# Two small opening loads issued from ScalarE's DMA queue instead of SyncE's

## The chip, the cores and the metric

The kernel runs on one core of a Trainium2 chip. The metric is the device time of one execution in microseconds (us). Before the change the median of three runs is 630.89 us (629.98 to 631.63). The profiled execution whose trace is read below took 630.4 us, of which 628.6 us lie between its first and its last instruction (its span).

## The reference

One layer of a latent generator, for 1024 latent tokens and 256 context tokens of width 1024. A conditioning vector gives shift, scale and gate of an adaptive norm; the normed tokens go through one wide input projection, whose columns feed a neighbourhood attention and a gated short convolution; an output projection and the residual follow.

```python
def adaln(cond, w_ada, b_ada):
    m = jax.nn.silu(cond) @ w_ada + b_ada
    return jnp.split(m, 3, axis=-1)
...
    shift, scale, gate = adaln(c, w_ada, b_ada)
    shift_c, scale_c, gate_c = adaln(c_ctx, w_ada, b_ada)
    h = rmsnorm(x, norm_g) * (1 + scale[:, None]) + shift[:, None]
    hc = rmsnorm(ctx, norm_g) * (1 + scale_c) + shift_c
    q, k, v, za, u, bg, cg, zc = jnp.split(h @ w_in, SPLIT_POINTS, axis=-1)
    ...
    attn = neighbourhood_attention(q, k, heads(v), kc, vc, rpb) * jax.nn.silu(za)
    conv = gated_short_conv(u, bg, cg, zc, conv_w, conv_b)
    x_new = x + gate[:, None] * (jnp.concatenate([attn, conv], axis=-1) @ w_out)
```

## The kernel before

Everything is one long program without loops on the chip. Products are made of high and low halves in three matmuls (`mm3`), so TensorE has most of the work. The stages are: the opening (modulation, norms, transposes of `x`, and the first projection columns, up to about 60 us), the rest of the projection (to about 300 us), attention with convolution work filled in between, and the output projection.

The change lies in the opening. There each engine's order is the order of the code (`strict` chains each engine's instructions). What matters of it:

- `vec` holds 56 rows of 128 numbers: the conditioning vectors, the norm gain, biases and convolution weights. `ci` holds the 128x128 identity and two more columns. Both are loaded once, at lines 117 and 118.
- `load_slab(m, j)` loads a block of `w_ada` (`slab`). The first two blocks come as two halves each, so four transfers of 512 KB open the stream; then come tiles of `x` (`xx`, 512 KB each) and pieces of `w_in` (`wr`, 192 KB).
- On TensorE, `keep_clock(6)` runs six matmuls on zeros (`warm`); then one transpose of `vec` with the identity of `ci` writes `tr` (called `pv` in the code); then `keep_clock(7)` runs seven more; then `products(0, 0)` and `products(0, 1)` multiply the first blocks of `w_ada` with the conditioning vector.
- VectorE copies the transposed `vec` to `vecT`; ScalarE makes the SiLU of the conditioning vectors from it (`c2`, and its copies `c4` and `c0`), which the products need.
- ScalarE squares each tile of `x` with a running sum (`square`, tile `sqj`), VectorE and GpSimd make the inverse root (`root`, tile `xss`), VectorE scales the tile in place (`norm`, `xx<-xx,xss`), TensorE transposes it with the identity (`tr<-ci,xx`), ScalarE and VectorE apply the modulation (`turn`, writing `h` and `hw`), and `first_columns` makes the first projection matmuls (`acc<-h,w`).
- `row_copy(0)` on VectorE (`rw<-tr`) takes the products out of PSUM, between the first and the second `root`; `modulation(0, rw)` turns the row (`tr<-ci,rw`) and writes `ab`, which `turn` needs.

Each transfer counts up one of eight shared completion counters, and a transfer is issued only when the earlier one on its counter has landed; a counter is given to each transfer when the program is built. So at most eight of these transfers are under way.

```python
    vec = cp.tile([P, P], F32, name="vec")
    nvec = vecs.shape[0]
    sp.dma_start(vec[:nvec], vecs)
    sp.dma_start(ci, cst[:, 0:P + 2])
...
    load_slab(0, 0)
    load_slab(0, 1)
    load_x(range(4))
    load_chunks([0])
```

Of the kernel before, what the change touches and what calls it, by code (L numbers as in the profile page):

```python
# [19 lines left out]
P = 128  # L20
# [19 lines left out]
def body(tc, es, x, ctxt, w_ada, b_ada, w_in, q_g, k_g, rpbr, w_out, vecs, cst, out):  # L40
# [21 lines left out]
    pe, act, dve, pool = every = [ordered(e) for e in (nc.tensor, nc.scalar, nc.vector, nc.gpsimd)]  # L62
    sp = ordered(nc.sync)
# [48 lines left out]
    ci = cp.tile([P, P + 2], F32, name="ci")  # L112
    ident = ci[:, 0:P]

    vec = cp.tile([P, P], F32, name="vec")
    nvec = vecs.shape[0]
    sp.dma_start(vec[:nvec], vecs)
    sp.dma_start(ci, cst[:, 0:P + 2])
    few = cp.tile([P, 8], F32, name="few")
    pool.memset(few[:, 0:4], -0.5)  # L120
    pool.memset(few[:, 4:5], 1.0)
# [1427 lines left out]
```

## Time and profile before

| quantity | value |
|---|---|
| median of three runs | 630.89 us (629.98 to 631.63) |
| the profiled execution | 630.4 us |
| its span, first to last instruction | 628.6 us |
| TensorE busy (matmul) | 621.7 us, 99% |
| VectorE busy | 433.5 us, 69% |
| ScalarE busy | 326.5 us, 52% |
| DMA queue of SyncE (q1) | 97516 packets, 114.24 MB |
| DMA queue of ScalarE (q10) | 6208 packets, 11.05 MB |

PE is TensorE's matmul side and PEld its weight loads; DVE is VectorE, ACT ScalarE, POOL GpSimd. SPq and ACTq rows are DMA instructions in the queues of SyncE and ScalarE; the time of such a row is the time that issuing takes, not the transfer's. A matmul's row gives its time from start to end, and matmuls overlap, so the step from one start to the next is shorter than a row's mean. Most instructions are emitted through one helper and stand under L55; they are told apart by the tiles. A bracket at the end of a row gives how long the engine stood idle before it and what ended that.

### The profile page before, as it was taken

What the parts mean: (1) busy time and instruction counts of PE and PEld (TensorE: products, weight loads), DVE (VectorE), ACT (ScalarE), POOL (GpSimd) and SP (SyncE); (2) the same over time, 40 slices, a digit from 0 to 9 for tenths busy, and PEclk for the clock granted to TensorE, in tenths of its full rate; (3) what the DMA queues carried; (4) which work ended last, traced back from release to release, by engine and by line L of the source; (5) the groups of instructions that cost most, each with busy time, mean ns of one, the idle gap of its engine ahead of it and who ended that gap; (6) DMA issues with size and microseconds to landing.
All of it is one profiled execution on the core that took longest, in us unless ns stands there. A gap on an engine that the chain in (4) does not pass through costs nothing.

```text
span 628.6 us, 10005 instructions
## 1 busy us (share of the span) xinstructions
PE 621.7 (99%) x3487; PEld 538.5 (86%) x3488; DVE 433.5 (69%) x889; ACT 326.5 (52%) x712; POOL 77.6 (12%) x102
## 2 busy tenths in 40 slices
PE   8999999999999999999999999999999999999998
PEld 3577899999999999888888888888888888888887
DVE  1887858866866855568897879988998865594111
ACT  3777835524625545346576568566774845450000
POOL 1305014113223221100000000000000002004200
PEclk9999999999999999999999999999999999999999
DMA  8983737967784995885474553775542235963621
GB/s 316 347 282 124 178 111 259 286 204 244 236 293 137 302 320 181 298 264 214 144 238 140 192 172 127 214 254 181 190 136 76 61 93 163 357 226 121 213 102 50
DMA packets 104030, 126.45 MB, mean 201 GB/s; under 512 B 10689, under 2 KB 70553, under 8 KB 102700
## 3 DMA queue, kind: packets, MB, share of 16 engines
q1 hardware_dynamic: 97516, 114.24, 55.3%
q10 hardware_dynamic: 6208, 11.05, 5.6%
q0 software_dynamic: 256, 0.54, 0.3%
q8 instruction: 27, 0.44, 0.3%
q14 instruction: 23, 0.19, 0.1%
HBM read 89.04 MB, written 39.04 MB: 204 GB/s over the span
## 4 chain that ended last, share of the span: by engine, by line
PE 96%; DMA 2%; SPq 1%; ACT 0%; issue 0%; DVE 0%; ACTq 0%
PE pu L55 29%; PE pacc L55 21%; PE po L55 8%; PE acc L55 6%; PE pout L75 5%; PE pout L74 5%; PE pout L76 5%; PE tr L55 4%; PE cacc L55 4%; PE pss L55 3%; PE pc L55 2%; PE pmx L55 2%; DMA xx<-in_x 2%; PE trA L55 1%; PE trB L55 1%; SPq L55 1%
## 5 line engine op out<-in xcount | busy, mean ns | idle before, releaser
L55 PE MATMUL pu<-h,uh 128*128 128x512 f32 x544 | 170.0, 394 | 0.0
L55 PE MATMUL pacc<-w,h 128*128 128x384 f32 x768 | 138.4, 337 | 0.0
L55 PEld LDWEIGHTS pacc<-w,h 128*128 128x128 f32 x768 | 132.7, 188 | 0.2
L55 PEld LDWEIGHTS pu<-h,uh 128*128 128x128 f32 x544 | 97.6, 188 | 16.8 <-ACT zs L55 0.2
L55 PE MATMUL pu<-h,ul 128*128 128x512 f32 x272 | 106.6, 392 | 0.0
L55 PEld LDWEIGHTS pu<-h,ul 128*128 128x128 f32 x272 | 51.1, 188 | 11.2
L55 POOL TENSOR_TENSOR ss<-ss,few 128x4 f32<-128x4 f32 (+1 forms) x40 | 41.9, 1049 | 124.8 <-DVE ss L55 124.8
L75 PE MATMUL pout<-wol,yh 128*128 128x512 f32 (+2 forms) x136 | 51.6, 379 | 0.0
L74 PE MATMUL pout<-woh,yh 128*128 128x512 f32 (+2 forms) x136 | 51.5, 379 | 0.0
L76 PE MATMUL pout<-woh,yl 128*128 128x512 f32 (+2 forms) x136 | 50.8, 379 | 0.0
L55 PE MATMUL acc<-h,w 128*128 128x512 f32 x144 | 38.1, 404 | 0.8 <-ACT h L55 0.8
L55 ACT ACTIVATE sq<-pacc 128x256 f32<-128x256 f32 x32 | 12.4, 388 | 47.5 <-PE pacc L55 43.7
L55 DVE TENSOR_REDUCE rm<-pmx 128x2 f32<-128x256 f32 (+1 forms) x33 | 13.8, 417 | 32.7 <-PE pmx L55 32.6
L55 ACT COPY mg<-pmx 128x256 f32<-128x256 f32 (+1 forms) x33 | 12.1, 366 | 46.4 <-PE pmx L55 42.0
L55 DVE TENSOR_TENSOR mx<-mx,sb 128x372 f32<-128x372 f32 (+2 forms) x64 | 31.9, 498 | 1.9
L55 PE MATMUL po<-phl,v 128*65 128x276 f32 (+2 forms) x192 | 32.0, 269 | 0.0
L55 DVE TENSOR_REDUCE ss<-sq 128x4 f32<-128x260 f32 (+1 forms) x40 | 15.7, 392 | 23.6 <-ACT sq L55 23.6
L55 ACT ACTIVATE qn<-pacc,ss 128x64 f32<-128x64 f32 x128 | 30.2, 333 | 3.0 <-POOL ss L55 3.0
L55 PEld LDWEIGHTS acc<-h,w 128*128 128x128 f32 x144 | 25.5, 188 | 6.5 <-ACT h L55 1.2
L1479 DVE TENSOR_TENSOR ot<-pout,xr 128x512 f32<-128x512 f32 (+2 forms) x9 | 5.7, 632 | 35.4 <-PE pout L76 33.3
L55 ACT COPY sc<-pc 128x512 f32<-128x512 f32 x32 | 18.8, 589 | 21.1 <-PE pc L55 21.0
L74 PEld LDWEIGHTS pout<-woh,yh 128*128 128x128 f32 x136 | 25.6, 188 | 4.7
(159 smaller groups left out, 1194.4 us busy)
## 6 DMA issues: line engine op xcount, KB each, us to landing
uraw<-in_w_in SPq DMA_DIRECT2D x34, 256.0 KB
q_d<-qs SPq DMA_DIRECT2D x32, 256.0 KB
k_s<-k_d SPq DMA_DIRECT2D x8, 1024.0 KB
q_s<-q_d SPq DMA_DIRECT2D x16, 512.0 KB
wr<-in_w_in SPq DMA_DIRECT2D x40, 192.0 KB
slab<-in_w_ada SPq DMA_DIRECT2D x6, 1024.0 KB
v_d<-vs SPq DMA_DIRECT2D x20, 260.0 KB
v<-v_d SPq DMA_DIRECT2D x16, 325.0 KB
```

The costliest lines, as they stand in the source:

```text
L55: i = emit(*a, **kw)
L74: i = pe.matmul(ps, ah, bh, start=first, stop=False)
L75: pe.matmul(ps, ah, bl, start=False, stop=False)
L76: pe.matmul(ps, al, bh, start=False, stop=last)
L1479: dve.tensor_tensor(ot[:, c], ps[c.start][:, c], xr[:, c], ALU.add)
```

## The change

The two small loads, of `vec` and of `ci`, are issued by ScalarE instead of SyncE. Sizes, destinations and everything behind them stay.

```diff
     vec = cp.tile([P, P], F32, name="vec")
     nvec = vecs.shape[0]
-    sp.dma_start(vec[:nvec], vecs)
-    sp.dma_start(ci, cst[:, 0:P + 2])
+    act.dma_start(vec[:nvec], vecs)
+    act.dma_start(ci, cst[:, 0:P + 2])
     few = cp.tile([P, 8], F32, name="few")
```

First, SyncE's queue at the program's start, before the change. `slab` is a block of `w_ada`, `xx` a tile of `x`, `wr` a piece of `w_in`; "waits DMAHW0" means that the transfer is issued when the earlier one on counter 0 has landed.

```order
L117 DMA vec_113<-in_vecs 56x128
L118 DMA ci_112<-in_cst 128x130
L55 DMA slab_156<-in_w_ada 128x4x256 x2
L55 DMA slab_159<-in_w_ada 128x4x256 x2
L55 DMA xx_162<-in_x 128x1024
L55 DMA xx_164<-in_x 128x1024
L55 DMA xx_166<-in_x 128x1024 [waits DMAHW0_49]
L55 DMA xx_168<-in_x 128x1024 [waits DMAHW1_49]
L55 DMA wr_170<-in_w_in 128x3x128 [waits DMAHW2_49]
L55 DMA xx_172<-in_x 128x1024 [waits DMAHW3_49]
```

And the same queue after the change:

```order
L55 DMA slab_156<-in_w_ada 128x4x256 x2
L55 DMA slab_159<-in_w_ada 128x4x256 x2
L55 DMA xx_162<-in_x 128x1024
L55 DMA xx_164<-in_x 128x1024
L55 DMA xx_166<-in_x 128x1024 [waits DMAHW0_49]
L55 DMA xx_168<-in_x 128x1024 [waits DMAHW1_49]
L55 DMA wr_170<-in_w_in 128x3x128 [waits DMAHW2_49]
L55 DMA xx_172<-in_x 128x1024 [waits DMAHW3_49]
```

The two small loads are gone from the head, and the first block of `w_ada` stands first. The waits read alike, but the counters behind them are dealt out anew: before, counters 0 to 5 went to `vec`, `ci` and the four halves of the blocks in that order; now `vec` has 0, the halves of the first block 1 and 2, `ci` 3, and the halves of the second block 4 and 5. So the fourth tile of `x` (`xx_168`) now waits for the first half block instead of for `ci`, the first `wr` for the second half block instead of the first, and the fifth tile (`xx_172`) for `ci` instead of the second half block.

Second, ScalarE's queue from its start, before:

```order
L124 ACT_TABLE_LOAD
L124 CAST oner_119<-few_116 128x1 [waits Pool_49]
L55 ACT_TABLE_LOAD
L55 ACTIVATE c2_125<-vecT_124 128x2x8 [waits DVE_49]
L55 CAST c4_211<-c2_125 128x8x2 [waits Activation_49]
```

And after:

```order
L117 DMA vec_113<-in_vecs 56x128
L118 DMA ci_112<-in_cst 128x130
L124 ACT_TABLE_LOAD
L124 CAST oner_119<-few_116 128x1 [waits Pool_49]
L55 ACT_TABLE_LOAD
L55 ACTIVATE c2_125<-vecT_124 128x2x8 [waits DVE_49]
L55 CAST c4_211<-c2_125 128x8x2 [waits Activation_49]
```

The two loads stand ahead of both table loads and of the SiLU `c2`; they wait for nothing. The order on TensorE, VectorE and GpSimd is the same as before.

## The prediction

> **What bounds the kernel now.** I read the page first, then busy time by stage, then the chain of waits through the opening, then single engines there. The page says how much each engine works:
>
> ```profile
> span 628.6 us, 10005 instructions
> PE 621.7 (99%) x3487; PEld 538.5 (86%) x3488; DVE 433.5 (69%) x889; ACT 326.5 (52%) x712; POOL 77.6 (12%) x102
> ```
>
> TensorE (PE) has work almost always. Busy time in stretches (start:end, length, then each engine) says where it has not:
>
> ```profile
> 0.00:20.00 20.00, 17.27 (x71) 6.74 (x72) 5.26 (x17) 9.44 (x17) 4.41 (x12) 1.00 0.91 335
> 20.00:60.00 40.00, 39.23 (x228) 28.42 (x228) 32.17 (x54) 28.98 (x43) 10.47 (x11) 1.00 0.67 231
> 60.00:160.00 100.00, 99.96 (x569) 92.95 (x568) 72.60 (x177) 51.50 (x155) 22.71 (x33) 1.00 0.70 211
> ```
>
> From 60 us PE is full: 99.96 of 100 us. A shift of its start is therefore handed on to the end one to one; nothing later has time to absorb it. The opening is another matter: part of the 17.27 us there are zeros that only keep PE going. The chain of waits shows what really sets it (start, length, what):
>
> ```profile
> 0.75 0.46 SPq L117
> ...
> 1.26 0.37 SPq L118
> ...
> 1.67 0.43 SPq L55
> ...
> 5.10 9.96 DMA xx<-in_x
> ...
> 15.14 1.16 ACT sqj L55 x2
> ...
> 20.03 0.79 ACT h L55
> ...
> 20.86 4.58 PE acc L55 x18
> ```
>
> The two small loads stand at the head of this chain, then SyncE's other issues, then 9.96 us in which a tile of `x` waits its turn and comes in, then squares, modulation, and at 20.86 the first projection matmuls. The last columns of the stretches are the busy share of the DMA engines and GB/s:
>
> ```profile
> 2.20:2.90 0.70, 0.70 (x3) 0.29 (x2) 0.00 (x0) 0.68 (x2) 0.00 (x0) 1.00 0.58 117
> 3.30:4.00 0.70, 0.70 (x2) 0.00 (x0) 0.00 (x0) 0.22 (x1) 0.00 (x0) 1.00 0.87 259
> 6.00:11.00 5.00, 5.00 (x24) 1.85 (x23) 0.00 (x0) 0.00 (x0) 0.00 (x0) 1.00 1.05 390
> 21.00:28.00 7.00, 7.00 (x30) 4.05 (x30) 6.14 (x12) 4.33 (x9) 2.77 (x3) 1.00 1.10 380
> ```
>
> While the small loads run, around 2.5 us, the engines carry 117 GB/s; once the blocks of `w_ada` flow they are full, at 380 to 390 GB/s, until 28 us. So the opening is a stream of bytes at full rate, and what counts is when that stream begins.
>
> **What the change gives.** SyncE issues its first block at 1.67 us; with the small loads gone it can at 0.75, where the first of them stood. That is 0.92 us. The bytes of the two loads still have to be moved, and now beside the blocks instead of ahead of them:
>
> ```profile
> ci<-in_cst SPq DMA_DIRECT2D x1, 65.0 KB
> vec<-in_vecs SPq DMA_DIRECT2D x1, 28.0 KB
> ```
>
> 93 KB at 390 GB/s are 0.24 us. The stream is thus ahead by 0.92 - 0.24 = 0.68, say 0.7 us. Behind it the new counters change little: `xx_168` now waits for a half block, but by then six transfers of 512 KB are under way, 1.3 us each at 390 GB/s, so the engines don't run dry. I count that at nothing; the cover is those six transfers.
>
> [...]
>
> **What the change costs.** First ScalarE. Its rows at the start:
>
> ```profile
> 0.74 1.28 ACT L124 ACT_TABLE_LOAD   x1 [0.74 <-PEq L1532]
> 2.24 1.28 ACT L55 ACT_TABLE_LOAD   x1
> 4.69 0.22 ACT L55 ACTIVATE c<-vecT 128x16 f32<-128x16 f32 x1 [1.17 <-DVE vecT L55]
> ...
> 12.59 1.06 ACT L55 ACTIVATE sqj<-xx 128x1024 bf16<-128x1024 f32 x1 [7.33 <-DMA xx<-in_x]
> ```
>
> Two issues, 0.46 + 0.37 us plus gaps by SyncE's rows, push the table loads back by some 0.92 us. ScalarE was free at 3.52 and is now free at 4.44, while the SiLU starts at 4.69: hidden by 0.25 us. (The last row is the first square, which had waited 7.33 us for `x`.) If issuing took twice as long, the SiLU would come 0.7 us late; that too is hidden, because the products need its result only at 6.70. So: nothing.
>
> Second, the arrival of `vec` and `ci`. This is the cost that the trace of before does not show. PE's rows:
>
> ```profile
> 1.38 2.74 PE L55 MATMUL acc<-warm 128*128 128x512 bf16 x6 [1.38 <-POOL c L55]
> 4.05 0.35 PE L55 MATMUL tr<-ci,vec 56*128 56x56 f32 x1
> 4.34 2.43 PE L55 MATMUL acc<-warm 128*128 128x512 bf16 x7
> 6.70 7.07 PE L55 MATMUL tr<-slab,c 128*2 128x256 f32 x32
> ```
>
> PE is in order: six matmuls on zeros, the transpose of `vec`, seven more, then 32 products, which end at 13.77. The bytes of the two loads were moved by about 2.9 (the stretch of 117 GB/s) and PE came to them at 4.05. The slack is those 1.15 us less what it takes until a landing is seen, which no row gives; I take 0.8. How late may the transpose be? VectorE's rows:
>
> ```profile
> 13.84 0.67 DVE L55 COPY rw<-tr 2x512 f32<-2x512 f32 x1
> 15.07 0.15 DVE L55 TENSOR_SCALAR xss<-xss 128x1 f32<-128x1 f32 x1 [0.57 <-ACT sqj L55]
> 16.32 0.15 DVE L55 TENSOR_SCALAR xss<-xss 128x1 f32<-128x1 f32 x1 [0.41 <-ACT sqj L55]
> 17.58 0.15 DVE L55 TENSOR_SCALAR xss<-xss 128x1 f32<-128x1 f32 x1
> 18.86 0.75 DVE L55 TENSOR_SCALAR xx<-xx,xss 128x1024 f32<-128x1024 f32 x1 [0.44 <-POOL xss L55]
> ```
>
> The row copy, held by the products, ends at 14.51, and VectorE then waits 0.57 us for the square of the second tile and 0.41 for the third. Both waits come from the stream of `x`. Without them the way from the row copy to the scaling of the fourth tile at 18.86 would take 3.79 - 0.41 = 3.38 us, so the products alone allow it at 14.51 + 3.38 = 17.89. The chain through `x` sets 18.86 now and 18.86 - 0.7 = 18.16 after the change. Hence the rule that I use for all cases: if PE's transpose starts later than 4.05 by d, the start of the projection moves by the larger of -0.7 and d - 0.97 us. The gain shrinks from d = 0.27 on and is gone at d = 0.97.
>
> Now bounds for d. From below: none, 0, if the small loads go ahead of the blocks as before; PE itself isn't there sooner. From above, the nearest rows are two stores of 128 KB from ScalarE's queue, one with SyncE's queue idle and one with it loaded (issue, then the queue's packets in the stretch 306.2:307.1 and 403.9:406.1):
>
> ```profile
> 305.10 0.51 ACTq L1103 DMA_DIRECT2D o_d<-ob  x1
> q10 hardware_dynamic: 80, 0.13, 62.8%
> 401.49 0.45 ACTq L1103 DMA_DIRECT2D o_d<-ob  x1
> q10 hardware_dynamic: 82, 0.13, 15.9%
> q1 hardware_dynamic: 255, 0.54, 78.8%
> ```
>
> The first needs at most 2.0 us from issue to the end of its stretch. The second has no packet from 401.4 to 403.9, where only q1 moves (the last row), and is then spread up to 406.1: 4.6 us. Being beside a loaded queue cost it up to 2.6 us. Taken whole, that makes d = 2.6 - 0.8 = 1.8 and a loss of 0.8 us. But there SyncE had several loads queued ahead; at 0.75 us there is nothing but what SyncE issues in the same half microsecond. I take 0 to 1.0 us of delay, d up to 0.2, and so a cost of nothing; the upper end stays in the range.
>
> [...]
>
> What follows the opening: one more wait for the stream, by ScalarE on a block of `w_ada`,
>
> ```profile
> ACT slabh L55 <- DMA slab<-in_w_ada: 2.6, 1, 2.6
> ```
>
> ends with the stream and so moves by the same 0.7 us; PE is late for nothing new there.
>
> **The sum.** 630.4 of the profiled execution less 0.7 is 629.7; the median shown stands 0.5 above that execution, so the forecast is 630.2. About 0.3%, 1.9 us, is what a measurement of this kernel can tell from no change; the forecast lies well inside that.
>
> **The rivals.** (a) The start of the stream is given back: the transpose is late by about 1 us (the two loads share the engines with the first blocks, d about 0.97), or the two queues issue no faster together than one did. Then 630.9, the median as it was. For it: the second store above. Chance 0.2.
>
> (b) Slower: ScalarE's loads are served behind the four halves already in SyncE's queue. These are 2.1 MB, 5.4 us at 390 GB/s; with the first packets about 1.1 us after the issue at 0.75 they end at 7.2, `ci` is seen 0.3 later at 7.5, d is 3.5 and the loss 2.5 us: 633.4. It decides from d = 2.9 on, where the loss passes 1.9 us. For it: the second store got no packet at all for 2.4 us. Against it: that store's queue had waited behind older loads, and here both queues start empty. A pause of PE could add to it: the six matmuls on zeros take 2.74 us, over 0.4 each, and the products 7.07 / 32 = 0.22, so TensorE ran at half pace until then. [...] Chance 0.17.
>
> (c) Faster than forecast by far: PE's idle time before 20.86 goes as well. In the stretch up to 20 us PE lacks 2.7 us, of which 1.4 lie before its first matmul; with the 0.7 that makes at most 2.0 us: 628.9. Against it: this idle time is the wait for `x`, which the stream sets. Chance 0.08, the median's own scatter in it.
>
> (d) The change doesn't do what it says: excluded by the order shown, since SyncE's first instruction is a block of `w_ada`.
>
> **How the numbers follow.** The forecast has 0.55, (a) 0.2, (b) 0.17, (c) 0.08. Faster by over 0.3% needs (c): 0.1 with a lucky median. Slower by over 0.3% needs (b): 0.16. The rest, 0.74, is the same. The range goes from the full 0.92 us of gain and 0.9 of scatter (the runs shown reach from 629.98 to 631.63), 630.9 - 0.92 - 0.9 = 629.1, to the loss of 0.8 by the second store and 0.7 of scatter, 632.4; (b) is left out.
>
> **What would show it.** In the profile after, SyncE's first block is issued at about 0.75 us, ScalarE's first table load at about 1.66, PE's `tr<-ci,vec` still at about 4.05, and the products still from 6.70 to 13.77; the first square of `x` moves from 12.59 to about 11.9, the first `acc<-h,w` from 20.86 to about 20.2, and the span to about 627.9. I am wrong if `tr<-ci,vec` starts after 4.3, if the first square does not move, or if the projection starts earlier and the end doesn't follow.

## The result and the profile after

The changed kernel takes 632.68 us (median of 6 runs, 632.6 to 634.04) against 630.45 us before (6 runs): ratio 1.0039, 95% interval 1.0026 to 1.0052. It is slower by some 2.2 us, just outside the forecast range. Run again beside other kernels (e10 below) the ratio was 1.0060 (1.0038 to 1.0082), 4.0 us slower.

The profiled execution took 632.6 us; its span grew from 628.6 to

```profile
span 630.8 us, 10006 instructions
```

The chain of waits through the opening, after the change (start, length, what):

```profile
0.74 0.68 ACTq L117
...
1.46 4.88 DMA ci<-in_cst
...
6.48 0.33 PE tr L55
6.80 3.10 PE acc L55 x7
9.90 7.11 PE tr L55 x32
...
22.93 4.58 PE acc L55 x18
```

The tile of `x` is gone from the chain. In its place stands `ci`: issued at 1.46, it holds TensorE (PE) until 6.48. Then come the seven matmuls on zeros and the 32 products, and the projection starts at 22.93 instead of 20.86, 2.07 us later. The same on PE itself, with the wait in the bracket:

```profile
1.38 2.74 PE L55 MATMUL acc<-warm 128*128 128x512 bf16 x6 [1.38 <-POOL c L55]
6.48 0.33 PE L55 MATMUL tr<-ci,vec 56*128 56x56 f32 x1 [2.35 <-DMA ci<-in_cst]
6.74 3.17 PE L55 MATMUL acc<-warm 128*128 128x512 bf16 x7
9.83 7.17 PE L55 MATMUL tr<-slab,c 128*2 128x256 f32 x32
```

PE pauses 2.35 us, and the seven matmuls on zeros, 2.43 us before, now take 3.17: all of them run at the slow pace of the first six (2.74 for six). The queues' packets in the stretches 1.5:4.1 and 4.1:6.1 (packets, MB, share of the 16 engines) say where `ci` was:

```profile
q1 hardware_dynamic: 463, 0.47, 53.4%
q10 hardware_dynamic: 70, 0.03, 6.5%
q1 hardware_dynamic: 667, 0.66, 95.5%
q10 hardware_dynamic: 144, 0.07, 11.7%
```

Up to 4.1 us ScalarE's queue (q10) had moved `vec` alone, 0.03 MB, while SyncE's (q1) moved 0.47 MB, which is nearly its first half block (512 KB, 0.52 MB). Only then came `ci`, 0.07 MB, and from there on the two queues moved side by side. SyncE had begun to issue its second half block too before ScalarE began with `ci`:

```profile
1.25 0.50 SPq L55 DMA_DIRECT2D slab<-in_w_ada  x1
1.46 0.37 ACTq L118 DMA_DIRECT2D ci<-in_cst  x1
```

So `ci` came behind one transfer of SyncE's queue, not behind all whose issue had begun before its own. SyncE and ScalarE did what the change says:

```profile
0.74 2.77 SPq L55 DMA_DIRECT2D slab<-in_w_ada  x4
1.85 1.28 ACT L124 ACT_TABLE_LOAD   x1 [1.85 <-issue]
7.09 0.22 ACT L55 ACTIVATE c<-vecT 128x16 f32<-128x16 f32 x1 [2.45 <-DVE vecT L55]
10.84 1.06 ACT L55 ACTIVATE sqj<-xx 128x1024 bf16<-128x1024 f32 x1 [3.19 <-DMA xx<-in_x]
```

The stream of `x` did come earlier (first square at 10.84, before at 12.59), but the chain no longer runs through it: it goes through `ci` and the products. ScalarE, with both issues done, still waited 2.45 us for `vecT` before its SiLU.

### The profile page after: what moved, and what is told of

The parts are those of the page before. It is cut to its first block, busy times and chain, and to the rows that moved or that the text cites. A ratio compares the mean times of both kernels' runs of the same rounds, so it can differ in the third digit from the quotient of the medians.

```text
span 630.8 us, 10006 instructions
## 1 busy us (share of the span) xinstructions
PE 622.6 (99%) x3488; PEld 538.5 (85%) x3488; DVE 433.7 (69%) x889; ACT 326.7 (52%) x712; POOL 78.8 (12%) x102
## 4 chain that ended last, share of the span: by engine, by line
PE 96%; DMA 1%; issue 1%; DVE 1%; ACT 1%; POOL 0%; ACTq 0%
PE pu L55 29%; PE pacc L55 21%; PE po L55 8%; PE acc L55 6%; PE pout L76 5%; PE pout L74 5%; PE pout L75 5%; PE tr L55 5%; PE cacc L55 4%; PE pss L55 3%; PE pc L55 2%; PE pmx L55 2%; PE trA L55 1%; DMA ci<-in_cst 1%; PE trB L55 1%
## 5 line engine op out<-in xcount | busy, mean ns | idle before, releaser
L76 PEld LDWEIGHTS pout<-woh,yl 128*128 128x128 f32 x136 | 25.6, 188 | 5.0 <-DVE yl L1454 0.3
L55 ACT COPY sc<-pc 128x512 f32<-128x512 f32 x32 | 18.8, 590 | 21.2 <-PE pc L55 21.1
```

The lines of the kernel that those rows point to most:

```text
L55: i = emit(*a, **kw)
L76: pe.matmul(ps, al, bh, start=False, stop=last)
```

## The experiments

The theories: A, a small load is served behind the SyncE transfer that stands ahead of it; B, the cost is ScalarE's own delay by issuing; C, sharing the DMA engines packet by packet makes the load late. Times below are "ratio to the kernel before on the same chip (95% interval)"; before was 629.74 to 629.80 us there. "First projection matmul" is the first `acc<-h,w`, at 20.86 before.

**e1: only `vec` from ScalarE.**

```diff
-    act.dma_start(ci, cst[:, 0:P + 2])
+    sp.dma_start(ci, cst[:, 0:P + 2])
```

> Only vec goes to ScalarE's queue; ci stays first on SyncE's. Theory A (a load is served behind the SyncE transfers that were issued before it): both loads are issued at about 0.75 us, ahead of any block, so the transpose of vec starts at 4.05 to 4.2, the products at 6.7, the first projection matmul 0.2 to 0.6 us before 20.86, and the time is 0.2 to 0.6 us below the kernel before. Theory B (issuing on ScalarE delays its table loads and the SiLU, and that costs): ScalarE issues one load instead of two, so about half of the 2.2 us stays. Theory C (the two queues share the DMA engines packet by packet, and that alone makes the small load late): vec is late by some 0.5 us at most, no loss.

Measured 629.64 us, 1.0001 (0.9987 to 1.0015). The transpose stands at 4.06 without a wait, the first projection matmul comes at 19.66.

```profile
4.06 0.35 PE L55 MATMUL tr<-ci,vec 56*128 56x56 f32 x1
```

No loss, against B, which asked for some 1.1 us, just above the interval. The small gain of A isn't shown; the interval does not exclude it.

**e2: only `ci` from ScalarE.**

```diff
-    act.dma_start(vec[:nvec], vecs)
+    sp.dma_start(vec[:nvec], vecs)
```

> Only ci goes to ScalarE's queue; vec stays first on SyncE's. Theory A: ci is issued at 0.75 us and the first half block only at 1.25, so ci is served first: transpose at 4.05 to 4.3, time 0.2 to 0.6 us below the kernel before. Theory B: half of the 2.2 us stays. Theory C: ci's packets share the engines with the first half block from about 2.3 us on and are as late as in the changed kernel less the 0.7 us by which they are issued earlier: transpose at about 5.8, slower by about 1 us.

Measured 630.35 us, 1.0011 (0.9991 to 1.0030), too wide an interval to decide on B. The transpose again stands at 4.06 with the same row, the first projection matmul at 19.37. So `ci` on ScalarE's queue is not late as such: as the first transfer of its queue it was served in time (its 0.07 MB had been moved by 2.7 us), and C's 5.8 us did not come.

**e3: `ci` ahead of `vec`, both from ScalarE.**

```diff
-    act.dma_start(vec[:nvec], vecs)
     act.dma_start(ci, cst[:, 0:P + 2])
+    act.dma_start(vec[:nvec], vecs)
```

> Both loads on ScalarE's queue, ci ahead of vec. Theory A: ci comes early and vec, now issued second, is served behind the first half block; it is smaller, so the transpose of vec starts at 5.5 to 6.3 instead of 6.48 and the kernel is 1.2 to 2.1 us slower than before. Theory B: same 2.2 us as the changed kernel, whatever the order. Theory C: the larger load is early, the smaller one only a little late: transpose at about 4.5 to 5, about no change against the kernel before.

Measured 632.7 us, 1.0036 (1.0022 to 1.0050), 2.9 us lost where A expected 1.2 to 2.1. PE's row shows that now `vec` is what it waits for:

```profile
6.05 0.32 PE L55 MATMUL tr<-ci,vec 56*128 56x56 f32 x1 [1.93 <-DMA vec<-in_vecs]
```

In these two traces whichever load is second in ScalarE's queue is late: PE waits 2.35 us for `ci` in the changed kernel and 1.93 for `vec` here. The transpose at 6.05 is A's outcome; C's, no change, is out.

**e4: all thirteen matmuls on zeros ahead of the transpose.**

```diff
-    keep_clock(6)
+    keep_clock(13)
     pv = tr()
...
-    keep_clock(7)
```

> The changed kernel with all thirteen matmuls on zeros ahead of the transpose of vec, so that TensorE does not pause while ci is under way. If the pause held the clock back: the second matmul pace (0.216 us from start to start) is reached before 6.5 us instead of at about 10, the transpose starts at about 6.5, the products at about 7.4 at full pace, end at about 14.4, and the kernel is 0.2 to 0.5 us faster than before. If the clock does not depend on the pause: the products start at about 7.9 after thirteen matmuls at the slow pace and run at it until about 10; the time is 0.3 to 1 us above the kernel before.

Measured 630.61 us, 1.0013 (1.0002 to 1.0025). `ci` is as late as in the changed kernel, but:

```profile
1.38 5.11 PE L55 MATMUL acc<-warm 128*128 128x512 bf16 x13 [1.38 <-POOL c L55]
6.46 0.24 PE L55 MATMUL tr<-ci,vec 56*128 56x56 f32 x1
7.25 7.07 PE L55 MATMUL tr<-slab,c 128*2 128x256 f32 x32 [0.56 <-ACT c L55]
```

Thirteen take 5.11 us, where six and seven at the slow pace take 2.74 and 3.17: the full pace came within them. With the zeros moved to where PE has to wait anyway, the products start at 7.25 instead of 9.83 and most of the loss is gone: 0.8 us is left. The gain that I expected is not there; the interval lies above 1, although in the trace the first projection matmul comes at 20.25, before the 20.86 of the kernel before.

**e5: the pause filled, the rest kept.**

```diff
-    keep_clock(6)
+    keep_clock(12)
     pv = tr()
```

> The changed kernel with six more matmuls on zeros ahead of the transpose of vec, so that TensorE is busy while ci is under way; the seven behind it stay. The transpose starts at about 6.5 us as in the changed kernel; what goes is the pause. If the pause cost its own share by the clock, the seven and the products run at the full pace: products from about 8.2 to 15.3, first projection matmul at about 21.3 to 21.8, which is 0.4 to 1 us later than in the kernel before instead of 2.07; the rest, 1.1 to 1.7 us, was the clock's share. If the lateness of ci alone is the cause, it stays at about 22.9.

Measured 631.66 us, 1.0026 (1.0014 to 1.0039).

```profile
6.62 0.35 PE L55 MATMUL tr<-ci,vec 56*128 56x56 f32 x1
6.90 1.83 PE L55 MATMUL acc<-warm 128*128 128x512 bf16 x7
8.66 7.07 PE L55 MATMUL tr<-slab,c 128*2 128x256 f32 x32
21.66 2.53 PE L55 MATMUL acc<-h,w 128*128 128x512 f32 x9 [0.76 <-ACT h L55]
```

The transpose is even later than in the changed kernel, now because the twelve matmuls ahead of it last until then (it has no wait of its own), yet the seven matmuls take 1.83 us instead of 3.17, and the projection starts 0.80 us later than before instead of 2.07. Between these two traces the pause thus had its own share of about 1.3 us. The times agree only loosely: 1.9 us lost in the median, and the interval meets that of the changed kernel.

**e6: the first block as one transfer of 1 MB.** In `load_slab`:

```diff
-        n = 2 if m == 0 else 1
+        n = 2 if (m, j) == (0, 1) else 1
```

> The changed kernel with the first block of w_ada as one transfer of 1 MB instead of two of 512 KB. Theory A (ci is served behind the SyncE transfer that was issued just before it, whatever its size): ci's packets begin only after that megabyte, at about 5.9 instead of 4.2 us; the transpose starts at about 8.1 and the first projection matmul at 24 to 25, 3 to 4 us later than in the kernel before. Theory C (packet by packet): no change against the changed kernel, transpose at about 6.5.

Measured 634.22 us, 1.0068 (1.0051 to 1.0085), 4.5 us lost. Packets in the stretches 1.5:5.0 and 5.0:6.5:

```profile
q1 hardware_dynamic: 903, 0.92, 82.4%
q10 hardware_dynamic: 70, 0.03, 4.7%
q1 hardware_dynamic: 502, 0.50, 93.8%
q10 hardware_dynamic: 144, 0.07, 15.5%
```

Again `ci` waits until nearly all of the one transfer ahead has been moved, 0.92 MB of it. In time it was less than expected (5.0 instead of 5.9 us, the transpose at 6.77 instead of 8.1, the first projection matmul at 23.19 instead of 24 to 25). The stretches 7:8, 8:9 and 10:12 show the clock; the third column from the end is its granted share:

```profile
7.00:8.00 1.00, 1.00 (x6) 0.49 (x6) 0.56 (x3) 0.53 (x3) 0.00 (x0) 0.88 1.09 388
8.00:9.00 1.00, 1.00 (x4) 0.16 (x2) 0.00 (x0) 0.00 (x0) 0.00 (x0) 0.50 1.08 427
10.00:12.00 2.00, 2.00 (x8) 0.71 (x7) 0.15 (x1) 1.20 (x3) 0.00 (x0) 0.71 1.04 424
```

In this execution the granted share read 1.00 from 1 to 7 us; behind a pause of 2.65 us it read 0.88 from 7 to 8 us, in the seven matmuls on zeros, 0.50 from 8 to 10, 0.71 from 10 to 12, in the products, and 1.00 again from 12 to 14. The 32 products took 7.99 us against 7.07 before. In the traces of the kernel before, the changed kernel, e5 and e8 this column reads 1.00 from 1 to 14 us, also while seven matmuls on zeros take 3.17 us in the changed kernel against 1.69 in e8; it does not show the slow start, which is read from the matmuls' own times. The start at 23.19 is only 0.26 us later than in the changed kernel. Of the 4.5 us lost in the median, the opening of this trace explains 2.3; another 1.7 was lost behind 517 us (see the next section).

**e7: no ScalarE, but `ci` behind the first half block on SyncE's queue.** From the kernel before:

```diff
-    sp.dma_start(vec[:nvec], vecs)
-    sp.dma_start(ci, cst[:, 0:P + 2])
...
+    sp.dma_start(vec[:nvec], vecs)   # ahead of load_slab(0, 0)
...
+            if (m, j, i) == (0, 0, 0):   # in load_slab, behind the first half
+                sp.dma_start(ci, cst[:, 0:P + 2])
```

> All on SyncE's queue again, in the order vec, first half block, ci, second half block; nothing on ScalarE's. Theory A (it is the place behind the half block that counts, not the queue): the transpose starts at 5.2 to 6 us, the first projection matmul 0.5 to 1.7 us later than in the kernel before, without any work on ScalarE's queue. Theory B (ScalarE's issuing is the cost): no loss; the transpose would start at about 4.1.

Measured 631.7 us, 1.0021 (1.0007 to 1.0036).

```profile
5.12 0.32 PE L55 MATMUL tr<-ci,vec 56*128 56x56 f32 x1 [0.99 <-DMA ci<-in_cst]
5.37 3.17 PE L55 MATMUL acc<-warm 128*128 128x512 bf16 x7
8.47 7.25 PE L55 MATMUL tr<-slab,c 128*2 128x256 f32 x32
```

A loss of the same kind without ScalarE's queue: B is out. It is the place behind the half block that costs, and behind a pause of 0.99 us the slow pace held through all seven matmuls. The first projection matmul comes at 21.65, 0.79 later than before; the median lost 1.95.

**e8: the first block in four transfers of 256 KB.** From the changed kernel, in `load_slab`:

```diff
-        n = 2 if m == 0 else 1
+        n = (4 if j == 0 else 2) if m == 0 else 1
```

> The changed kernel with the first block of w_ada in four transfers of 256 KB. If the two queues are served in turn, one transfer of each, ci waits for the first 256 KB only: its packets begin at about 3.3 us, the transpose starts at about 5.4 and the first projection matmul at 21.3 to 22. If transfers are served in the order in which they were issued, ci (issued at 1.46 us) stands behind two quarters and nothing changes against the changed kernel: transpose at about 6.5. Theory C: no change either.

Measured 632.1 us, 1.0028 (1.0012 to 1.0044). Packets in the stretches 1.5:3.0 and 3.0:4.5:

```profile
q1 hardware_dynamic: 187, 0.19, 40.2%
q10 hardware_dynamic: 70, 0.03, 7.8%
q1 hardware_dynamic: 461, 0.44, 90.5%
q10 hardware_dynamic: 144, 0.07, 16.0%
```

```profile
5.01 0.24 PE L55 MATMUL tr<-ci,vec 56*128 56x56 f32 x1 [0.89 <-DMA ci<-in_cst]
5.19 1.69 PE L55 MATMUL acc<-warm 128*128 128x512 bf16 x7
```

`ci` starts after 0.19 MB. With e6 and the changed kernel there are three sizes: 0.19, 0.47 and 0.92 MB moved ahead of `ci` where the transfer ahead had 0.26, 0.52 and 1.05 MB. The issue of the second quarter had begun before that of `ci` (1.25 and 1.45 us), and only one quarter was served first: in these three traces the transfers of the two queues began in turn, one of each, the next when most of the one ahead had been moved. Which part of the chip takes the turns, no run shows. In the profiled execution (630.32 us) the pause of 0.89 us did no harm to the pace (1.69 us for the seven), and the first projection matmul came at 20.05, earlier than before and than the 21.3 to 22 expected; the median is 1.8 us above that execution. That other executions ran the seven at the slow pace, as e7 did (3.17 us), fits, and so does a spread behind 517 us, but no trace of them was taken.

**e9: both loads in one transfer from ScalarE.** `vecs` is laid beside the identity in one array:

```diff
-    act.dma_start(vec[:nvec], vecs)
-    act.dma_start(ci, cst[:, 0:P + 2])
+    act.dma_start(cv, cst[:, 0:2 * P + 2])
```

> Both small loads in one transfer of 132 KB from ScalarE's queue (the vectors are laid beside the identity in one array). If only the second transfer of ScalarE's queue is served behind a SyncE block and the first goes ahead at once, this one is served from about 1.8 us on, beside the first half block, and has landed before 4.05: no pause of TensorE, the transpose at 4.05 to 4.5, the first projection matmul 1 to 1.5 us before that of the kernel before, and a time 0.3 to 1 us below it. If its bytes share the engines with the half block and that makes it late, the transpose starts after 4.5 us, the pause costs the clock in part of the executions, and the time is 0 to 1.5 us above the kernel before.

Measured 631.12 us, 1.0017 (1.0002 to 1.0033).

```profile
4.33 0.35 PE L55 MATMUL tr<-ci 56*128 56x56 f32 x1 [0.21 <-DMA ci<-in_cst]
4.61 2.67 PE L55 MATMUL acc<-warm 128*128 128x512 bf16 x7
```

First in its queue, the transfer is late by 0.21 us only. Up to 3.0 us only this queue moves bytes (stretch 1.5:3.0), though SyncE's first half block was issued at 0.74 as well; here the block came second:

```profile
q10 hardware_dynamic: 79, 0.08, 77.6%
```

The expected gain did not come. The time is that of the second expectation, a small loss, but its condition, a transpose after 4.5 us, is not met in the trace, and the first projection matmul at 20.20 is earlier than before. In this execution the loss came behind 517 us (next section).

**e12: the same transfer at the head of SyncE's queue.**

```diff
-    act.dma_start(cv, cst[:, 0:2 * P + 2])
+    sp.dma_start(cv, cst[:, 0:2 * P + 2])
```

> The same single transfer at the head of SyncE's queue, nothing on ScalarE's. One issue of about 0.45 us is saved, so the blocks start some 0.4 us earlier than before, and the transfer is served first: transpose at 4.05, first projection matmul 0.2 to 0.5 us earlier, time 0 to 0.5 us below the kernel before.

Measured 629.87 us, 0.9996 (0.9979 to 1.0014). The transpose stands at 4.05, the first projection matmul at 19.48; there is no difference that the times could tell.

**e11: e2 with fewer matmuls on zeros.**

```diff
-    keep_clock(7)
+    keep_clock(4)
```

> vec first on SyncE's queue, ci on ScalarE's, and four instead of seven matmuls on zeros behind the transpose. With vec and ci on different queues both were there at 4.05 us, and the first square of x came 1.5 us earlier than before; the products, behind seven matmuls on zeros, were what set the start. With three fewer the products start 0.6 to 1.2 us earlier, the first projection matmul at about 18.8 to 19.1, and the time is 0.3 to 1.3 us below the kernel before. If the clock needs those matmuls, part of the products runs at half pace and nothing is gained.

Measured 629.23 us, 0.9990 (0.9979 to 1.0000). The products start at 5.47 at full pace (7.07 us for the 32, as in e2), 0.91 us earlier than in e2, but the first projection matmul comes at 19.42, no earlier than there (19.37) and later than the 18.8 to 19.1 expected: the products no longer set it. It has the lowest median of these kernels, 0.5 us below before, at the edge of what the interval tells.

**e10: the changed kernel again.** No edit.

> The changed kernel once more, on this chip. If the 2.2 us are the lateness of ci together with the pause of TensorE: 1.8 to 3 us above the kernel before, transpose of vec at 6.3 to 6.7 us, full pace of the matmuls not before 8 us. If the first measurement was a matter of its chip, less than 1 us.

Measured 633.75 us, 1.0060 (1.0038 to 1.0082). The transpose stands at 6.41 behind a wait of 2.29 us for `ci`, the seven matmuls take 3.17 us again, the products 7.56, and the first projection matmul comes at 23.24. The mechanism is the same; the loss of 4.0 us is more than the 1.8 to 3 expected, and the 2.4 us at the start of the projection do not cover it.

## Why the prediction was wrong

The stream starts 0.92 us earlier: right, SyncE's first block is issued at 0.74, and the first square moved even further than the 0.7 us forecast, by 1.75. More than 0.92 cannot come from the issue. In e12 the first half block was issued only 0.47 earlier than before and the first square came at 10.89, 1.70 earlier; of all traces the one before has the latest first square. So `x` was probably late in that one execution; it is the only trace of the kernel before, and the cause stays open.

ScalarE's issues cost nothing: right, though with a smaller margin than I reckoned. Its first table load moved to 1.85 instead of 1.66, because issuing `vec` took it 0.68 us and not 0.46. It was free at 4.64, just before the 4.69 of its SiLU in the kernel before; here it stood free for 2.45 us until `vecT` was there.

The step that failed is the size of d, the delay of PE's transpose. I took "0 to 1.0 us of delay, d up to 0.2"; it was 6.48 - 4.05 = 2.43, more than even the bound of 1.8 from the two stores. I argued that at 0.75 us SyncE has nothing queued ahead but what it issues in the same half microsecond. That half microsecond holds a transfer of 512 KB, and e6 and e8 show that `ci` waits for just this one, at 1 MB and at 256 KB as well. The place in the order was the question, and I had answered it with rows of another place, as a time.

The second fault is a term left out of the sum. I named the slow pace, but only as an addition to rival (b). The seven matmuls and the products took 3.17 + 7.17 with starts at 6.74 and 9.83, so that the products end at 17.00 instead of 13.77: 3.23 us later, 0.8 of it from the pace.

The rule itself held: 3.23 - 0.97 = 2.26 us of loss, measured 2.07 at the first projection matmul and 2.2 at the end of the span. How far a shift of that start goes through is seen on VectorE: one row near 517 us and its last row (before, then the changed kernel):

```profile
517.56 0.69 DVE L55 TENSOR_TENSOR tb<-tb,zs 128x512 f32<-128x512 f32 x1
625.84 0.29 DVE L1479 TENSOR_TENSOR ot<-pout,xr 128x128 f32<-128x128 f32 x1 [2.07 <-PE pout L76]
519.53 0.69 DVE L55 TENSOR_TENSOR tb<-tb,zs 128x512 f32<-128x512 f32 x1
628.01 0.29 DVE L1479 TENSOR_TENSOR ot<-pout,xr 128x128 f32<-128x128 f32 x1 [2.07 <-PE pout L76]
```

From the first projection matmul to the row near 517 us all fourteen traces take 496.6 to 496.75 us: up to there the shift goes through one to one. From that row to the last they take 108.28 (the kernel before, the least of all) to 109.99 us (e6, from 519.80 to 629.79); e9 takes 109.70, and the two traces of the changed kernel 108.48 and 109.00. So the last stage adds up to 1.7 us of its own, which differs between two traces of one kernel. In e6 TensorE waits there once, 1.1 us for ScalarE's `yh`, in the kernel before not at all; what sets the spread is not shown. In e1, e2, e11 and e12 the traces show the start of the projection 1.2 to 1.5 us earlier, and the times show 0.5 us at most. The profiled execution before, 630.4 us, lies 0.6 above the medians before of the experiments, so its start at 20.86 may be late by about that; with one trace of the kernel before I cannot say.

Rival (b) had the right place for `ci` and the wrong depth: one half block ahead, not four. Its threshold, d = 2.9, was too high, since the slow pace adds 0.8 (the seven matmuls took 3.17 instead of 2.43 us, the products 7.17 instead of 7.07). Rival (a) had the transpose late by 0.97 instead of 2.43, and no slow pace.

The measured 2.43 and e3 decide against theory C, packet by packet, for the start of the second transfer of a queue: in the changed kernel that came only when 0.47 of the 0.52 MB ahead had been moved. Once begun, `ci` did share the engines with SyncE's queue (0.07 beside 0.66 MB from 4.1 to 6.1 us).

## What to carry to other kernels

Before moving a small load to another queue, ask which large transfer is issued beside it and who waits for the load: the second transfer of another queue did not get past a block that was issued at the same time, and the gain in issuing (0.92 us here) became a loss of 2.2 us or more. If a load gates an engine, make it the first of its queue: e1 and e2 lost nothing that the times could tell (e9 lost 1.4 us in the median, in its trace behind 517 us). A smaller block ahead of it brought the load earlier in the trace of e8, but no better median. Where matmuls on zeros stand ahead of the work so that it starts at full pace, place them where TensorE has to wait, ahead of the dependent instruction and not behind it: in e4 the products started at 7.25 instead of 9.83 and took 7.07 us, and 0.8 us of the loss was left.

## What the runs showed of the hardware

- Two transfers from ScalarE's queue beside SyncE's: the second was served only after 0.19, 0.47 and 0.92 MB of the SyncE transfer ahead (0.26, 0.52 and 1.05 MB; e8, the changed kernel, e6). In the changed kernel and in e8 the issue of a further SyncE transfer had begun before its own (1.25 against 1.46 and 1.45 us), and it did not wait for that one: there the transfers began in turn. In e9 SyncE's first block moved nothing until 3.0 us, behind ScalarE's transfer of 132 KB, of which 0.08 MB had been moved.
- A pause of TensorE in the first 7 us cost more than itself in five of the six traces that have one of 0.9 to 2.7 us: the seven matmuls behind it took 3.17 us at the slow pace in the changed kernel, e3, e7 and e10, against 1.83 with the pause filled (e5) and 1.91 to 2.43 without a pause (e1, e2, before). In e6 the granted clock fell to 0.50 between 8 and 10 us, and the products took 7.99 us. In e8 a pause of 0.89 us cost nothing more: the seven took 1.69.
- Issuing `vec` took ScalarE 0.68 us in the changed kernel, and SyncE 0.46 before.
- The stage behind 517 us took 108.28 to 109.99 us in the fourteen traces, while the stretch ahead of it, from the first projection matmul on, took 496.6 to 496.75 in all of them.
